# Attention inside a decoder layer: projection tiles that take every fourth token, scores and exponents in one PSUM bank, a column of ones in v

## The chip, the cores and the metric

The kernel runs on one core of a Trainium2 chip. The time is device time in microseconds (us) from the first to the last instruction and what lies around them; three runs of the kernel before took 2241.93, 2246.85 and 2247.97 us. The engines of the core are PE (TensorE, matmuls; PEld is its weight load), DVE (VectorE), ACT (ScalarE), POOL (GpSimd) and SP (SyncE, which here issues nearly all DMAs). Each runs its own instructions in order.

## The reference, cut to what matters

One decoder layer on 2048 tokens of width 1024, in float32. The change touches only the attention half of the mixer: 8 heads of 64, and for every head three branches (window, dilation) = (128,1), (512,4), (2048,16). A query at position t attends to the keys at t, t-d, t-2d, ... back to t-window.

```python
DILATED_BRANCHES = ((128, 1), (512, 4), (2048, 16))
...
def dilated_branch(q, k, v, window, dil):
...
    qs, ks, vs = to_sub(q), to_sub(k), to_sub(v)      # tokens regrouped by residue mod dil
...
    s = jnp.einsum("bnqhd,bnkhd->bnhqk", qb, kw, preferred_element_type=jnp.float32)
...
    valid = ((dist >= 0) & (dist <= L))[None] & (kpos >= 0)
    s = jnp.where(valid[None, :, None], s, -jnp.inf)
    m = jnp.max(s, axis=-1, keepdims=True)
    e = jnp.exp(s - m)
    den = jnp.sum(e, axis=-1, keepdims=True)
    p = e / den
    lse = (m + jnp.log(den))[..., 0]
    o = jnp.einsum("bnqhk,bnkhd->bnqhd", p.astype(vw.dtype), vw)
```

The three branches of a head are then combined with weights that go with their denominators. Before the attention stand an RMS norm, the projection and a gated convolution, and behind it the output projection and a SwiGLU.

## The kernel before

Every float32 operand of a matmul is split into two float16 parts, high and low, and a product is three matmuls (high by high, high by low, low by high: `mm3_steps`, L187 to L189).

The kernel has four stages in time: norm and convolution (to about 240 us of the profile), the attention (projection of the first head pair to about 306 us, then four groups g of two heads to about 845 us), the output projection, and the feed-forward, which fills the rest.

`qkv_steps(g)` projects q, k and v of the two heads of group g. It goes over the tokens in four blocks of 512 (`i`), and in each block over four tiles (`j`) of 128 consecutive tokens: 24 matmuls of 384 columns whose weights are the tile's tokens (`xh[:, k, t]`) and whose moving side are the weights of the layer. ACT copies q and k out of PSUM (L456) and the high half of v (L458), DVE makes v's low half (L459), and SP stores v to DRAM (L463, rows of 128 float16: 64 high, 64 low). After four tiles come the norms of q and k: squares on POOL (L468), a sum and a reciprocal root on DVE, two products on POOL (L473, L476), the casts to float16 on DVE (L482, L483), the low halves on POOL (L484, L485), and six DMA transposes (L195, called at L488) that put the head dimension on the partitions: `qT`, `ka` (high part of k, held twice) and `kl` (low part of k over zeros; its buffers are called kb in the profile). All have the 2048 tokens in natural order along their free dimension.

`attn_steps(g)` does the attention of the group: for each head h the branches b in the order 1, 2, 0 (dilation 4, 16, 1), in blocks u of 128 queries. A step takes either two blocks with the previous and the own block of keys (256 columns each), or four blocks with the own keys alone (128 columns each, `four`): branch 2 throughout, and the first step of branch 1. There are 152 steps, 112 of them with two blocks. A step is: score matmuls into a PSUM bank `s` (L567 with the high, L568 with the low part of k; lhsT is the queries' block, rhs a slice of the keys); on DVE the mask, the scale and the row minimum, from `s` into an SBUF tile `sm` (L572); on ACT the exponent in `sm`, with its row sum (L577); then the float16 split and the transpose of the exponents. With two blocks the split goes through `eh` (L588 on ACT, L589 on DVE) and a DMA transpose into `et` (L590, recorded at L195); with `four` PE transposes `sm` into PSUM (L583) and ACT and DVE split it from there (L584, L585). Then 12 or 24 matmuls `av` (L596) multiply by v. Slices of the keys: branch 0 contiguous; branch 1 every 4th token (`tl[:, ...:4]`, 8 bytes apart); branch 2 every 16th (`tl[:, u::16]`, 32 bytes apart). Buffers: three PSUM banks `s`, three tiles `sm`, four each of `eh` and `et`.

Order: the Tile framework derives all semaphores from the tiles and puts the instructions of each engine in an order of its own with a timeline model. `attention_pairs` feeds it the steps of group g and, between them, the projection of group g+1 (a `yield` is three matmuls; `rate` yields per step), held back by `issue_after` so that it runs at most `lag` steps ahead. In the last group the filler is the last quarter of the convolution and the first output tiles. v comes back from DRAM per head and branch in `load_v`, one DMA each, two buffers.

Of the kernel before, what the change touches and what calls it, by code (L numbers as in the profile page):

```python
# [8 lines left out]
F32 = mybir.dt.float32  # L9
# [8 lines left out]
P = 128  # L18
S = 2048
# [10 lines left out]
class Builder:  # L30
# [167 lines left out]
    def run(self):  # L198
        tc, nc, A = self.tc, self.nc, self.A
        with ExitStack() as ctx:  # L200
# [4 lines left out]
            self.d_v = [dr.tile([2, S, P], F16, name=f"d_v{g}") for g in range(4)]  # L205
# [227 lines left out]
    def qkv_steps(self, g, st):  # L433
# [12 lines left out]
        for i in range(0, NT, 4):  # L446
            f = self.at.tile([P, 4, 4, HD], F32, name="qkf", bufs=2)
            for j in range(4):
                if j % 2 == 0:
                    vs = self.at.tile([P, 2, 2, 2, HD], F16, name="vs", bufs=2)  # L450
                t = slice(j * P, (j + 1) * P)
# [3 lines left out]
                                          lambda k: wh[:, k], lambda k: wl[:, k])  # L455
                nc.scalar.activation(f[:, j].rearrange("p a b -> p (a b)"), ps[:, 0:256], AF.Copy, scale=u)  # L456
                pv = ps[:, 256:384].rearrange("p (h d) -> p h d", h=2)
                nc.scalar.activation(vs[:, j % 2, :, 0], pv, AF.Copy, scale=2.0 ** -20)  # L458
                nc.vector.scalar_tensor_tensor(vs[:, j % 2, :, 1], pv, 2.0 ** -20, vs[:, j % 2, :, 0],  # L459
                                               op0=ALU.mult, op1=ALU.subtract)  # L460
                if j % 2 == 1:
                    for h in range(2):
                        nc.sync.dma_start(dv[h, (i + j - 1) * P:(i + j + 1) * P].rearrange("(t p) c -> p t c", p=P),  # L463
                                          vs[:, :, h].rearrange("p t x d -> p t (x d)"))
            n = self.at.tile([P, 16, HD], F32, name="qkn")
            ff = f.rearrange("p a b d -> p (a b) d")
            ss = self.at.tile([P, 16], F32, name="qk_ss")
            nc.gpsimd.tensor_tensor(n, ff, ff, op=ALU.mult)  # L468
# [11 lines left out]
            for h in range(2):  # L480
                q, k = n4[:, :, h], n4[:, :, 2 + h]
                nc.vector.tensor_copy(hl[:, h, :, 0], q)  # L482
                nc.vector.tensor_copy(hl[:, 2 + h], k.unsqueeze(2).broadcast_to([P, 4, 2, HD]))  # L483
                nc.gpsimd.tensor_tensor(hl[:, h, :, 1], q, hl[:, h, :, 0], op=ALU.subtract)  # L484
                nc.gpsimd.tensor_tensor(self.klz[:, h, :, 0], k, hl[:, 2 + h, :, 0], op=ALU.subtract)  # L485
            for src, dsts in ((hl, (*qT, *ka)), (self.klz, kl)):
                for n_, dst in enumerate(dsts):
                    self.transpose(dst[:, i * P:(i + 4) * P].rearrange("p (j t) -> p j t", j=4),  # L488
                                   src[:, n_].rearrange("p j x d -> p (j x d)"))
            yield  # L490
        st.update(qT=qT, ka=ka, kl=kl)

    def attn_steps(self, g, st):
# [6 lines left out]
        def load_v(h, b):  # L500
            dv = self.d_v[g][h]
            t = V[h, b] = self.vp.tile([P, NT, P], F16, name="v", bufs=2)
# [5 lines left out]
            else:  # L508
                nc.sync.dma_start(t, dv.rearrange("(t p) c -> p t c", p=P))
        for h, b in [(h, b) for h in range(2) for b in (1, 2, 0)]:  # L510
            qT, ka, kl = (st[x][h] for x in ("qT", "ka", "kl"))
            load_v(h, b)

# [631 lines left out]
```

## Time and profile before

| what | us |
|---|---|
| three runs | 2241.93, 2246.85, 2247.97 (median 2246.85) |
| profiled execution: whole / its span | 2241.81 / 2240.0 |
| PE, DVE, ACT, POOL busy in the span | 2127.7, 1491.1, 1022.5, 670.8 |
| attention from the first score to the last av and what follows it at once (306 to 845) | 539 |
| feed-forward and what lies between | 1395 |

How to read it: the first two rows are times of whole executions, and every duration and position in this document comes from the one that was profiled. Busy shares are averages over stages with different limits, so the stage from 306 to 845 us is looked at by itself. A matmul's own duration includes its way through the pipeline; what it costs on PE is the distance from its start to the next one's.

### The profile page before, as it was taken

Reading aid. Unit: us, or ns where it says so; the run is one execution under the profiler, and the core shown is the slowest. Engines: PE = TensorE matmul, PEld = TensorE weight load, DVE = VectorE, ACT = ScalarE, POOL = GpSimd, SP = SyncE. Lnnn points to the kernel's source line nnn. Section 1 sums busy time; section 2 is a strip of 40 time slices with the busy share of each in tenths; the row PEclk is TensorE's granted clock in tenths of the full one; section 3 lists DMA queues with packets and bytes.
Section 4 is the critical chain, followed back from the end, with each engine's and each line's share of the span. In section 5 each row is a group of like instructions: output and inputs, shape, how many; then the busy total and the mean of one; then the engine's idle time right before and its main releaser. Section 6 shows DMA issues by size and latency. Waiting matters only on the chain.

```text
span 2240.0 us, 33330 instructions
## 1 busy us (share of the span) xinstructions
PE 2127.7 (95%) x11816; PEld 1067.8 (48%) x11816; DVE 1491.1 (67%) x3412; ACT 1022.5 (46%) x2390; POOL 670.8 (30%) x524
## 2 busy tenths in 40 slices
PE   4899999999899979998799999999999999999999
PEld 2344556666565644443344444444444444444444
DVE  6587557878777667785576667676767565555554
ACT  6343236666566757563343333333343343343341
POOL 0000243445434111131221122221211235555463
PEclk9999999999899989999899999999999999999999
DMA  9767356978888988869633323333223455152342
GB/s 240 160 202 254 97 123 128 184 155 161 171 159 173 233 196 245 260 198 256 170 113 104 113 82 100 107 99 104 87 93 108 164 180 179 57 192 65 115 141 94
DMA packets 569703, 339.40 MB, mean 152 GB/s; under 512 B 372928, under 2 KB 522432, under 8 KB 567104
## 3 DMA queue, kind: packets, MB, share of 16 engines
q1 hardware_dynamic: 564528, 337.20, 57.0%
q8 instruction: 92, 1.51, 0.3%
q10 hardware_dynamic: 5008, 0.08, 0.1%
q14 instruction: 75, 0.61, 0.1%
HBM read 161.04 MB, written 107.48 MB: 120 GB/s over the span
## 4 chain that ended last, share of the span: by engine, by line
PE 67%; DMA 11%; DVE 10%; ACT 4%; SPq 4%; issue 4%; POOL 0%; DVEq 0%; ACTq 0%; POOLq 0%
PE ps L949 26%; PE ps L1067 18%; PE mm L187 5%; PE mm L188 5%; PE mm L189 5%; DMA et<-eh 3%; PE s L567 3%; PE s L568 3%; SPq L195 2%; PE av L596 2%; DMA wraw<-in_w_in_dram 1%; DMA wq<-in_w_up_dram 1%; DVE vm_a L92 1%; DVE w L860 1%; DVE hl L816 1%
## 5 line engine op out<-in xcount | busy, mean ns | idle before, releaser
L949 PEld LDWEIGHTS <-w 128*128 128x128 f16 x3696 | 363.3, 98 | 469.9 <-issue 23.9
L949 PE MATMUL ps<-b,w 128*128 128x512 f16 x2112 | 467.4, 383 | 15.0 <-ACT ka L799 8.4
L1067 PE MATMUL ps<-b,w 128*128 128x512 f16 x1848 | 399.3, 380 | 0.9 <-DVE s L1085 0.8
L949 PE MATMUL ps<-hb,w 128*128 128x512 f16 x1584 | 351.4, 383 | 9.2 <-DVE s L955 8.6
L1067 PEld LDWEIGHTS <-w 128*128 128x128 f16 x1848 | 180.7, 98 | 219.4 <-issue 1.4
L577 ACT ACTIVATE sm<-sm,u 128x256 f32<-128x256 f32 (+1 forms) x384 | 173.8, 455 | 68.7 <-DVE u L572 68.2
L842 POOL TENSOR_TENSOR t<-wq 128x512 f32<-128x512 f32 (+1 forms) x46 | 59.1, 1284 | 436.1 <-issue 205.7
L955 DVE TENSOR_TENSOR s<-ps,s 128x512 f32<-128x512 f32 x220 | 150.1, 683 | 47.0 <-PE ps L949 46.5
L572 DVE CUSTOM_DVE_ANT_0 sm<-s,mask,nkap 128x256 f32<-128x256 f32 (+1 forms) x384 | 144.1, 420 | 42.9 <-PE s L568 24.7
L187 PE MATMUL mm<-wq,b 128*128 128x384 f16 x512 | 172.4, 337 | 0.0
L188 PE MATMUL mm<-wq,b 128*128 128x384 f16 x512 | 171.9, 336 | 0.0
L189 PE MATMUL mm<-wq,b 128*128 128x384 f16 x512 | 171.6, 335 | 0.0
L1074 POOL TENSOR_TENSOR x<-x,s 128x512 f32<-128x512 f32 x72 | 103.0, 1432 | 186.2 <-DVE s L1085 130.0
L1075 DVE SCALAR_TENSOR_TENSOR x<-ps,a_u,x 128x512 f32<-128x512 f32 x96 | 71.9, 749 | 112.6 <-PE ps L1067 84.1
L568 PE MATMUL s<-kb,qT 128*128 128x256 f16 (+1 forms) x384 | 131.3, 358 | 3.0 <-DMA kb<-klz 3.0
L567 PE MATMUL s<-ka,qT 128*128 128x256 f16 (+1 forms) x384 | 130.1, 355 | 3.6 <-DVE u L572 2.2
L589 DVE TENSOR_TENSOR eh<-sm,eh 128x512 f16<-128x512 f32 (+1 forms) x112 | 100.3, 898 | 40.7 <-ACT eh L588 40.0
L187 PEld LDWEIGHTS <-b 128*128 128x128 f16 x768 | 77.3, 101 | 71.7 <-ACT b L721 7.5
L188 PEld LDWEIGHTS <-b 128*128 128x128 f16 x768 | 77.3, 101 | 65.0 <-issue 6.1
L189 PEld LDWEIGHTS <-b 128*128 128x128 f16 x768 | 76.8, 100 | 65.3 <-issue 4.5
L187 PE MATMUL cvx<-b,wq 128*128 128x512 f16 (+1 forms) x200 | 76.8, 388 | 30.4 <-ACT wq L145 24.6
L859 ACT CAST w<-t 128x512 f16<-128x512 f32 x88 | 53.6, 615 | 104.7 <-PE ps L949 82.2
(298 smaller groups left out, 3705.1 us busy)
## 6 DMA issues: line engine op xcount, KB each, us to landing
d_a<-a SPq DMA_DIRECT2D x88, 256.0 KB, 2.0
d_wd<-w SPq DMA_DIRECT2D x77, 256.0 KB, 2.0
wq<-d_a SPq DMA_DIRECT2D x64, 256.0 KB, 4.3
b<-d_wd SPq DMA_DIRECT2D x14, 1024.0 KB, 5.7
wraw<-in_w_in_dram SPq DMA_DIRECT2D x24, 512.0 KB, 6.7
v<-d_v SPq DMA_DIRECT2D x24, 512.0 KB, 5.0
d_h<-hl SPq DMA_DIRECT2D x24, 512.0 KB, 4.0
wq<-in_w_gate_dram SPq DMA_DIRECT2D x22, 512.0 KB, 5.3
```

What stands on the lines that cost most here:

```text
L187: self.pe = mm(ps, lhsT=lh(k), rhs=rh(k), start=k == ks[0], stop=False)
L188: mm(ps, lhsT=lh(k), rhs=rl(k), start=False, stop=False)
L189: mm(ps, lhsT=ll(k), rhs=rh(k), start=False, stop=k == ks[-1])
L567: nc.tensor.matmul(sp[:, at[u]], lhsT=q, rhs=cols(ka, u, pv), start=True, stop=False)
L568: nc.tensor.matmul(sp[:, at[u]], lhsT=q, rhs=cols(kl, u, pv), start=False, stop=True)
L572: nc.vector.tensor_tensor_reduce(sm[:, at[u]], sp[:, at[u]], self.mask[:, P - P * has_prev(u):256], accum_out=Ub[:, u, HD + 1:HD + 2], op0 ...
L577: nc.scalar.activation(sm[:, at[u]], sm[:, at[u]], AF.Exp, scale=-1.0, bias=Ub[:, u, HD + 1:HD + 2], accum_out=Ub[:, u, HD:HD + 1])
L589: nc.vector.tensor_tensor(eh[:, w:2 * w], sm[:, 0:w], eh[:, 0:w], op=ALU.subtract)
L949: nc.tensor.matmul(ps[self.BANK[n]], lhsT=w[:, x, k], rhs=b[:, y, k], start=first and k == 0 and q == 0, stop=k == 3 and q == 2, skip_grou ...
L955: nc.vector.tensor_tensor(t, x, y, op=ALU.add)
L1067: nc.tensor.matmul(ps[self.BANK[n]], lhsT=L[n][:, x, f], rhs=B[n][:, f, y], start=first and f == 0 and q == 0, stop=f == n_f - 1 and q == ...
L1074: nc.gpsimd.tensor_tensor(o, o, s_, op=ALU.add)
```

## The change

1. **Tokens by residue.** Tile j of a block of 512 now takes the tokens j, j+4, j+8, ... (`slice(j, 4 * P, 4)`), so the tile's weights are read with a step of 4 elements. k stays in that order: in each block of 512, `ka` and `kl` hold 128 tokens of residue 0, then of residue 1, and so on. q is transposed into small tiles `qp` and put back into natural order by a DVE copy, two for each block. The slices of the keys are new (`keys`): branch 1 reads contiguous runs of 128; branch 2 reads every 4th element; branch 0 reads runs of 32, in the order of residues, and three of its blocks in each head need two matmuls for each part where there was one. Branch 0 gets a mask with its columns in the new order, and its v is loaded with the partitions in the same order, by four DMAs in place of one.
2. **Exponents in the bank.** In a step with two blocks `sm` is now `s` itself: DVE writes the masked scores back into the PSUM bank, ACT puts the exponents there, and L588 and L589 read them from there. The bank is held until L589 has ended. Steps with four blocks keep `sm` in SBUF.
3. **Ones in v.** Each half of v has 65 columns, the last 1 in the high and 0 in the low half, written once into two fixed tiles `vs`. The av matmuls have 65 columns and give the row sum too, so the exponent has no `accum_out`; rows of v in DRAM have 260 bytes in place of 256.
4. **Work moved between engines.** The squares for the norm are made on ACT straight from PSUM, 16 tiles by 4 groups, in place of POOL's 16 products; the casts of q and k to float16 go from DVE to ACT.

```diff
@@ qkv_steps
-                if j % 2 == 0:
-                    vs = self.at.tile([P, 2, 2, 2, HD], F16, name="vs", bufs=2)
-                t = slice(j * P, (j + 1) * P)
+                vs = self.vs[j // 2]
+                t = slice(j, 4 * P, 4)
...
                 nc.scalar.activation(f[:, j].rearrange("p a b -> p (a b)"), ps[:, 0:256], AF.Copy, scale=u)
+                nc.scalar.activation(n[:, 4 * j:4 * j + 4].rearrange("p a b -> p (a b)"), ps[:, 0:256], AF.Square, scale=u)
...
-            nc.gpsimd.tensor_tensor(n, ff, ff, op=ALU.mult)
...
-                nc.vector.tensor_copy(hl[:, h, :, 0], q)
-                nc.vector.tensor_copy(hl[:, 2 + h], k.unsqueeze(2).broadcast_to([P, 4, 2, HD]))
+                nc.scalar.copy(hl[:, h, :, 0], q)
+                nc.scalar.copy(hl[:, 2 + h], k.unsqueeze(2).broadcast_to([P, 4, 2, HD]))
...
-            for src, dsts in ((hl, (*qT, *ka)), (self.klz, kl)):
+            four = [self.at.tile([P, 4, P], F16, name="qp", bufs=4) for _ in range(2)]
+            for src, dsts in ((hl, (*four, *ka)), (self.klz, kl)):
...
+            for h in range(2):
+                nc.vector.tensor_copy(qT[h][:, i * P:(i + 4) * P].rearrange("p (t j) -> p t j", j=4),
+                                      four[h].rearrange("p j t -> p t j"))
@@ load_v
-            t = V[h, b] = self.vp.tile([P, NT, P], F16, name="v", bufs=2)
+            t = V[h, b] = self.vp.tile([P, NT, 2 * HD + 2], F16, name="v", bufs=2)
...
-                nc.sync.dma_start(t, dv.rearrange("(t p) c -> p t c", p=P))
+                for r in range(4):
+                    nc.sync.dma_start(t[32 * r:32 * r + 32], dv.rearrange("(n p r) c -> r p n c", n=NT, r=4)[r])
@@ attn_steps
+            def keys(tl, u, prev):
+                k = tl.rearrange("p (n j t) -> p n j t", n=4, j=4)
+                n = u // 4
+                if b == 0:
+                    m = u % 4
+                    k = k.rearrange("p n j (m t) -> p n m j t", m=4)
+                    if prev and m == 0:
+                        return [k[:, n - 1, 3], k[:, n, 0]]
+                    return [k[:, n, m - prev:m + 1]]
+                if b == 1:
+                    return [k[:, n - prev:n + 1, u % 4]]
+                return [k[:, :, u % 4, u // 4::4]]
...
-                av = self.psav.tile([P, 4, HD], F32, name="av")
+                av = self.psav.tile([P, 4, HD + 1], F32, name="av")
...
-                        pv, q = has_prev(u), cols(qT, u, 0)
-                        nc.tensor.matmul(sp[:, at[u]], lhsT=q, rhs=cols(ka, u, pv), start=True, stop=False)
-                        nc.tensor.matmul(sp[:, at[u]], lhsT=q, rhs=cols(kl, u, pv), start=False, stop=True)
-                    sm = self.ep.tile([P, 512], F32, name="sm")
+                        pv = has_prev(u)
+                        hi, lo = keys(ka, u, pv), keys(kl, u, pv)
+                        w = (at[u].stop - at[u].start) // len(hi)
+                        for x in range(len(hi)):
+                            o = sp[:, at[u].start + x * w:at[u].start + (x + 1) * w]
+                            nc.tensor.matmul(o, lhsT=query(u), rhs=hi[x], start=True, stop=False)
+                            nc.tensor.matmul(o, lhsT=query(u), rhs=lo[x], start=False, stop=True)
+                    sm = self.ep.tile([P, 512], F32, name="sm") if four else sp
...
-                        nc.scalar.activation(sm[:, at[u]], sm[:, at[u]], AF.Exp, scale=-1.0, bias=Ub[:, u, HD + 1:HD + 2],
-                                             accum_out=Ub[:, u, HD:HD + 1])
+                        nc.scalar.activation(sm[:, at[u]], sm[:, at[u]], AF.Exp, scale=-1.0, bias=Ub[:, u, HD + 1:HD + 2])
...
-                        ops = [(et[:, q * nb + x], Vb[:, kb_, o:o + HD]) for q, o in ((0, 0), (0, HD), (1, 0))
+                        ops = [(et[:, q * nb + x], Vb[:, kb_, o:o + HD + 1]) for q, o in ((0, 0), (0, HD + 1), (1, 0))
...
-                nc.scalar.copy(Ub[:, u0:u0 + 4, 0:HD], av)
+                nc.scalar.copy(Ub[:, u0:u0 + 4, 0:HD + 1], av)
@@ attention_pairs
+        for name, pattern in (("mask", [[1, P]]), ("mask4", [[1, 4], [4, 32]])):
+            mask = self.at.tile([P, 256], F32, name=name)
+            nc.gpsimd.memset(mask, 0.0)
...
+        self.vs = [self.at.tile([P, 2, 2, 2, HD + 1], F16, name=f"vs{i}") for i in range(2)]
+        for t in self.vs:
+            nc.gpsimd.memset(t[:, :, :, 0, HD:HD + 1], 1.0)
+            nc.gpsimd.memset(t[:, :, :, 1, HD:HD + 1], 0.0)
```

43 lines of the change are left out of this document (23 added, 20 removed).

## The prediction

> **What bounds the kernel now.** I read the page's busy times first, then the windows of the attention (the whole stage lies between 306 and 845 us; the change touches nothing behind it), then the chain of work in that stage, then single matmuls by shape and in the timeline. The windows' columns are the stretch, its length, busy time and count of PE, PEld, DVE, ACT and POOL, then the clock granted to PE, the share of the DMA engines and GB/s.
>
> ```profile
> PE 2127.7 (95%) x11816; PEld 1067.8 (48%) x11816; DVE 1491.1 (67%) x3412; ACT 1022.5 (46%) x2390; POOL 670.8 (30%) x524
> ```
> ```profile
> 306.00:436.00 130.00, 125.36 (x1011) 82.27 (x1010) 93.62 (x328) 78.96 (x275) 48.08 (x35) 0.96 0.76 156
> 436.00:565.00 129.00, 124.51 (x1104) 83.45 (x1103) 104.01 (x339) 84.90 (x297) 60.06 (x40) 0.96 0.85 165
> 565.00:695.00 130.00, 120.58 (x1041) 78.35 (x1040) 97.18 (x325) 79.71 (x281) 58.47 (x41) 0.91 0.84 163
> 695.00:845.00 150.00, 128.83 (x1101) 78.61 (x1099) 105.29 (x398) 94.06 (x313) 38.11 (x26) 0.92 0.94 208
> ```
> ```profile
> by line: DMA et<-eh 13.0%; PE mm L187 11.9%; PE mm L189 11.8%; PE mm L188 11.7%; PE s L567 10.5%; PE s L568 10.5%; PE av L596 7.9%; PE pt L583 3.2%; ACT sm L577 2.3%; DVE eh L589 2.0%; issue 1.9%; ACT eh L588 1.5%; DVE sm L572 1.5%; DMA r<-
> ```
> ```profile
> q1 hardware_dynamic: 258846, 93.17, 84.7%
> ```
>
> Each group takes 129 to 150 us, and PE is busy for 499 of the 539 us. It is the first bound, and the chain agrees: scores (L567, L568) hold 21% of the stage, 113 us. The second bound stands close: the DMA engines are busy for 84.7% of 539 = 456 us (last row, the queue in this window), and the wait for `et` holds 13% of the chain. DVE (400 us) and ACT (338 us) have slack.
>
> **The scores: the term that carries the sum.** In the view by shape a score of 128 columns costs more than one of 256; the timeline shows why.
>
> ```profile
> L568 PE MATMUL s<-kb,qT 128*128 128x256 f16 x216 | 68.6, 335 | 3.0 <-DMA kb<-klz 3.0
> L567 PE MATMUL s<-ka,qT 128*128 128x256 f16 x216 | 68.0, 332 | 1.4 <-DMA ka<-qkhl 1.3
> L568 PE MATMUL s<-kb,qT 128*128 128x128 f16 x168 | 63.5, 388 | 0.0
> L567 PE MATMUL s<-ka,qT 128*128 128x128 f16 x168 | 63.4, 386 | 2.2 <-DVE u L572 2.2
> ```
> ```profile
> 306.13 0.28 PE L567 MATMUL s<-ka,qT 128*128 128x128 f16 x1
> ...
> 307.05 0.34 PE L187 MATMUL mm<-wq,b 128*128 128x384 f16 x1
> ...
> 309.02 0.39 PE L567 MATMUL s<-ka,qT 128*128 128x256 f16 x1
> ...
> 309.92 0.34 PE L187 MATMUL mm<-wq,b 128*128 128x384 f16 x1
> ```
> ```profile
> 363.72 0.27 PE L567 MATMUL s<-ka,qT 128*128 128x256 f16 x1
> ...
> 364.16 0.33 PE L187 MATMUL mm<-wq,b 128*128 128x384 f16 x1
> ```
> ```profile
> 405.26 0.33 PE L189 MATMUL mm<-wq,b 128*128 128x384 f16 x1
> 405.43 0.40 PE L567 MATMUL s<-ka,qT 128*128 128x128 f16 x1
> ...
> 407.33 0.35 PE L187 MATMUL mm<-wq,b 128*128 128x384 f16 x1
> ```
>
> From start to start: branch 0 (contiguous keys) does four scores of 256 columns in 0.44 us, 0.11 each; branch 1 (8 bytes apart) four in 0.90, 0.225 each, and eight of 128 columns in 0.92, 0.115 each; branch 2 (32 bytes apart) eight of 128 in 1.90, 0.238 each. So a column costs 0.43 ns contiguous, 0.88 at 8 bytes, 1.86 at 32. The change makes branch 1 contiguous and branch 2 a walk at 8 bytes. A head has 12 blocks of 256 and 4 of 128 columns in branch 1, 16 of 128 in branch 2, two matmuls each; 8 heads:
> - branch 1: 192 x (0.225 - 0.11) = 22 us, and 64 x (0.115 - 0.055) = 4 us;
> - branch 2: 256 x (0.238 - 0.115) = 31 us.
>
> Together 57 us less on PE. Branch 0 reads runs of 64 bytes: at 1.86 ns for each separate place (branch 2's price) a run's four 16-byte pieces take 7.4 ns, its 32 columns 13.8; I take nothing, upper bound a place's price for each run, 8 x 1.86 ns x 240 matmuls = 4 us. Its split blocks are two matmuls of half the columns, also nothing.
>
> The row at 8 bytes also meets a rule that says otherwise. The Trainium skill, "Advanced Engine Details and Errata", section "SBUF Cachelines", says that lines are 16 bytes and that two hits on a line absorb the access. By it branch 1 would have run at full speed before; the trace disagrees (0.225 against 0.11). By the rule branch 2's new walk would cost 0.055 and the gain there would be 47 us, not 31.
>
> **Weight loads with a step.** The projections' 1536 loads now step by 4 elements, and branch 2's queries still step by 16.
>
> ```profile
> 405.27 0.15 PEld L567 LDWEIGHTS <-qT 128*128 128x128 f16 x1
> 363.72 0.10 PEld L568 LDWEIGHTS <-qT 128*128 128x128 f16 x1
> ```
>
> A load with the widest step takes 0.15, a contiguous one 0.10. At 405.27 the wide one lay under L189's matmul, and the next started 0.17 after it, as everywhere: a 384-column matmul hides it. Without that cover, 1536 x 0.05 = 77 us at most; I take 0. Under branch 2's new 0.115 a load of 0.15 may show: up to 256 x 0.035 = 9 us, kept for the range.
>
> **av.** 24 matmuls of 64 columns take 0.70, 29 ns each; a 65th column adds 0.43 ns x 1800 = 0.8 us.
>
> ```profile
> 407.67 0.70 PE av L596 x24
> ```
>
> **Off PE.**
>
> ```profile
> L589 DVE TENSOR_TENSOR eh<-sm,eh 128x512 f16<-128x512 f32 x104 | 95.4, 920 | 36.4 <-ACT eh L588 35.8
> L577 ACT ACTIVATION_READ_ACCUMULATOR sm<-sm,u 128x1 f32 x384 | 72.9, 190 | 0.0
> L588 ACT CAST eh<-sm 128x512 f16<-128x512 f32 x104 | 63.9, 616 | 43.3 <-DMA et<-eh 42.8
> L468 POOL TENSOR_TENSOR qkn<-qkf 128x1024 f32<-128x1024 f32 x16 | 31.2, 1948 | 51.8 <-ACT qkf L456 51.8
> L456 ACT ACTIVATE qkf<-mm,uq 128x256 f32<-128x256 f32 x64 | 29.9, 468 | 73.6 <-PE mm L189 70.2 <-POOL mask L631 3.4
> L585 DVE TENSOR_TENSOR et<-pt,et 128x512 f16<-128x512 f32 x40 | 27.4, 686 | 13.7 <-ACT et L584 13.7
> L482 DVE CAST qkhl<-qkn 128x256 f16<-128x256 f32 x32 | 23.8, 779 | 9.7 <-POOL qkn L473 9.7
> L483 DVE CAST qkhl<-qkn 128x512 f16<-128x512 f32 x32 | 18.5, 616 | 0.6 <-POOL qkn L476 0.6
> ```
>
> ACT: minus 73 (the 384 accumulator reads), plus 64 squares at L456's 0.468 = 30, plus casts 32 x 0.47 and 32 x 0.62 (L456, L588) = 35: about level. DVE: minus 42 (L482, L483), minus 104 x (0.92 - 0.69) = 24 if the split reads PSUM as fast as L585 does, plus 32 copies of q at 0.4 to 0.7 (around L483) = 13 to 22: 44 to 53 us less. POOL: minus 31. None of these is the bound; they only shorten the way from a score to its `et`. The q copy adds its 0.6 us far ahead of use, and ACT now carries casts behind which exponents queue, 0.6 us at a time. Two POOL mask selects and five memsets more before the first projection: under 2 us, beside projections.
>
> SP: load_v of branch 0 issues four DMAs for one, 8 x 3 x 0.43 = 10 us of SP's time, ahead of transposes in its queue. Rows of v grow from 256 to 260 bytes, 1.6%. The transposes, most of the DMA work, stay as they are, so 456 us of DMA work remain.
>
> ```profile
> 441.42 0.43 SPq L504 DMA_DIRECT2D v<-d_v  x1
> ```
>
> **What is late next.** If all 57 us were turned into time the stage would last 482 us and the DMA share would be 456/482 = 0.95: above the 0.94 of the busiest window. At a share of 0.90, between the stage's mean (0.85) and that window, it lasts 507 us: 32 us less. The waits that show the limit are these, behind `eh`'s four buffers and behind `et`:
>
> ```profile
> ACT eh L588 <- DMA et<-eh: 42.8, 30, 4.6
> PEld L596 <- DMA et<-eh: 27.2, 17, 7.3
> ```
>
> In the last group (0.94 already) PE's saving of 14 us can hardly show; in the other three, 43 us of PE less, DMA work of 99 to 110 us each against some 110 us of PE. I take 30 us: 2241.8 - 30 = 2212 against the profiled execution. The runs' median is 5 us above it; I add half of that: **2214**.
>
> **The bank's new hold.** The other edit that can cost: a two-block step keeps its bank until L589.
>
> ```profile
> 433.86 0.27 PE L567 MATMUL s<-ka,qT 128*128 128x256 f16 x1
> ```
> ```profile
> 440.66 2.24 DVE L589 TENSOR_TENSOR eh<-sm,eh 128x512 f16<-128x512 f32 x2
> 442.82 0.47 DVE L572 CUSTOM_DVE_ANT_0 sm<-s,mask,nkap 128x256 f32<-128x256 f32 x1
> ```
>
> Scores made at 433.86 were masked only at 442.82, when L589 had set a tile `sm` free: three `sm` already pace the mask, and scores ran up to 9 us ahead. Now the score itself waits, and behind it on PE the projections and av. A hold without queues is 0.44 + 0.9 (two L572) + 1.0 (two L577) + 0.6 + 0.7 = 3.7 us, so three banks allow a step each 1.2 us, against 539/152 = 3.5 us now. Some waits will come in bursts; they are part of what keeps the gain under 57.
>
> ```profile
> 310.54 0.48 DVE L572 CUSTOM_DVE_ANT_0 sm<-s,mask,nkap 128x256 f32<-128x256 f32 x1
> 310.66 0.51 ACT L577 ACTIVATE sm<-sm,u 128x256 f32<-128x256 f32 x1 [0.73 <-DVE u L572]
> ```
>
> Here the second block's mask ran beside the first block's exponent. The Trainium skill, "PSUM — Partial Sum Buffer", section "PSUM bank collisions raise a hardware error", wants two engines kept out of one bank at a time; no run here shows it. By it 310.66 becomes 311.0, 0.36 us more in each of 112 holds.
>
> **Rivals.** (1) *All of it shows*: transposes keep up at a share of 0.95; 2185 to 2198. For it: DVE and POOL get out of the transposes' way. Against: no window is above 0.94. Chance 0.15. (2) *The DMA side is the bound already* (PE's time goes into waits for `et`, share at 0.85 to 0.88): 456/0.87 = 524, 15 us less; 2227 to 2242. For it: 70 us of waits for `et` in the two rows above; SP's 10 us more. Chance 0.23. (3) *Slower: the ring of three banks*. If a bank is held longer than 3 x 539/152 = 10.6 us on average, the ring and not PE sets the step: at 11 us 152 x 11/3 = 557, 18 us more, 2260. For it: the step above would have held its bank 9 + 3.2 us. Against: that is a burst; a hold without queues is a third. Chance 0.11. (4) *The strides don't pay* (branch 2 bound by the load at 0.15, branch 0 at its 4 us): PE saves 44 us, and by the same share of it, 30 of 57, some 23 show: 2219, inside the forecast's own 2198 to 2228, which has 0.51.
>
> **How the numbers follow.** Range: 2190 (half of rival 1) to 2247 (all of rival 2, the near end of 3). A measurement here tells about 0.3% from no change, 6.7 us. Faster by more than that: forecast 0.51, rival 1 0.15, half of rival 2, together 0.78; same 0.12; slower 0.10.
>
> **What would show it.** Right: from start to start branch 1 at 0.11 and 0.055, branch 2 at 0.115; projections still 0.162; no accumulator reads; L589 near 690 ns; DMA share near 0.90 in the attention; more waits for `et` on PE. Wrong: waits of PE's L567 for L589 of more than 30 us in total (ring), projections above 0.17 (loads), or a stage as long as before at a share of 0.85.

## The result and the profile after

| | before | after |
|---|---|---|
| median of six runs on one chip, us | 2246.15 (2241.93 to 2247.97) | 2225.47 (2224.36 to 2226.63) |
| ratio | | 0.9911, 95% interval 0.9899 to 0.9924 |
| profiled execution: whole / its span | 2241.81 / 2240.0 | 2224.36 / 2222.6 |
| first projection matmul / first score / end of the last av, us | 240.7 / 306.1 / 835.6 | 238.9 / 287.1 / 820.0 |

The change makes the kernel 20.7 us faster. The forecast was 2214, with 2190 to 2247 as its range: the sign is right, and 11 of the 32 us of gain are missing. In the two profiled executions the difference is 17.4 us.

First the page of the changed kernel, its busy times and its main DMA queue:

```profile
PE 2081.2 (94%) x11864; PEld 1080.7 (49%) x11864; DVE 1453.5 (65%) x3380; ACT 1030.2 (46%) x2134; POOL 624.6 (28%) x515
...
q1 hardware_dynamic: 564912, 337.46, 58.3%
```

PE lost 46.5 us of busy time (2127.7 before). The span lost only 17.4, so PE's idle time in the span rose by 29.1. That is the result in one line: most of what was saved on PE came back as waiting. The next rows are windows over the attention, from the first projection to the last av: first of the kernel before, then of the kernel after (columns as in the prediction).

```profile
240.70:835.60 594.90, 559.76 (x4630) 359.86 (x4629) 427.14 (x1463) 343.55 (x1187) 229.94 (x163) 0.95 0.80 165
```
```profile
238.90:820.00 581.10, 516.58 (x4689) 373.80 (x4687) 386.55 (x1429) 352.83 (x931) 185.09 (x155) 0.95 0.86 170
```

PE's idle time is the second number minus the third: 35.1 us before, 64.5 after. DVE and POOL became lighter, and none of DVE (387 of 581 us), ACT (353) and POOL (185) is busy enough to be the new bound by itself. I count from the first projection here, and not from the first score: the framework's plan of the changed kernel puts the first score 19 us earlier, and the stretch from first score to last av, which the prediction calls the stage, would hide the gain: it is 529 us before and 533 after.

The windows of the four groups after the change:

```profile
287.00:425.00 138.00, 129.38 (x1156) 98.59 (x1155) 88.56 (x345) 88.51 (x241) 43.31 (x38) 1.00 0.78 155
425.00:555.00 130.00, 110.90 (x1063) 83.32 (x1060) 92.81 (x328) 83.24 (x222) 47.11 (x36) 0.92 0.88 168
555.00:685.00 130.00, 114.81 (x1112) 85.22 (x1110) 93.66 (x334) 88.81 (x236) 52.41 (x43) 0.96 0.93 167
685.00:830.00 145.00, 124.25 (x1127) 78.98 (x1126) 101.97 (x385) 84.00 (x210) 29.08 (x20) 0.89 0.99 214
```

PE now waits 9, 19, 15 and 21 us in them (length minus PE's busy time); before it was 5, 4, 9 and 21 in the four windows of the prediction. The waits came where PE had been full, in the first three groups. The scores in the timeline (the columns are start, duration, engine and line), at the seam between branch 1 and branch 2:

```profile
330.89 0.27 PE L597 MATMUL s<-ka,qT 128*128 128x256 f16 x1
331.00 0.27 PE L598 MATMUL s<-kb,qT 128*128 128x256 f16 x1
331.10 0.28 PE L597 MATMUL s<-ka,qT 128*128 128x128 f16 x1
...
332.06 0.34 PE L189 MATMUL mm<-wq,b 128*128 128x384 f16 x1
332.24 0.32 PE L187 MATMUL mm<-wq,b 128*128 128x384 f16 x1
332.40 0.32 PE L188 MATMUL mm<-wq,b 128*128 128x384 f16 x1
```

From start to start a 256-column score of branch 1 takes 0.11 us; the eight of branch 2 take 0.96 (331.10 to 332.06), 0.12 each; a projection takes 0.16 to 0.18, as before. Over the whole stage the medians are 0.109, 0.056, 0.120 and 0.163 us (branch 1 with 256 and 128 columns, branch 2, projections); before they were 0.229, 0.117, 0.239 and 0.163.

The groups by shape after the change (busy, mean ns, then idle time before them and what ended it):

```profile
L603 DVE CUSTOM_DVE_ANT_0 s<-s,mask,nkap 128x256 f32<-128x256 f32 x216 | 101.3, 486 | 21.0 <-PE s L598 19.7
L608 ACT ACTIVATE s<-s,u 128x256 f32<-128x256 f32 x216 | 94.7, 456 | 63.5 <-DVE u L603 46.3 <-DVE qkr_y L50 5.3 <-DVE qkr_t L48 3.1
L626 PE MATMUL av<-v,et 128*128 128x65 f16 x1800 | 80.1, 197 | 41.3 <-DMA et<-eh 25.9 <-ACT u L629 9.9 <-DMA v<-d_v 2.9
L619 DVE TENSOR_TENSOR eh<-s,eh 128x512 f16<-128x512 f32 x104 | 70.8, 686 | 39.4 <-ACT eh L618 38.8
L597 PE MATMUL s<-ka,qT 128*128 128x256 f16 x192 | 49.2, 279 | 7.5 <-DVE eh L619 6.6 <-DVE u L603 0.8
L597 PE MATMUL s<-ka,qT 128*128 128x128 f16 x216 | 46.7, 266 | 3.5 <-DVE eh L619 3.5
L603 DVE DVE_READ_ACCUMULATOR2_ANT u<- 128x1 f32 x384 | 44.4, 116 | 0.0
L496 DVE COPY qT<-qp 128x512 f16<-128x512 f16 x32 | 24.2, 759 | 37.2 <-DMA qp<-qkhl 37.2
L485 POOL TENSOR_TENSOR qkhl<-qkn,qkhl 128x256 f16<-128x256 f32 x32 | 20.9, 674 | 3.5 <-ACT qkhl L483 3.5
```

L619 is the old L589: 686 ns in place of 920. No accumulator read is left on ACT. Scores wait 10 us in all for L619 to give a bank back, and `av` waits 41 us, 26 of them for `et`. The waits in the attention:

```profile
PEld L626 <- DMA et<-eh: 34.8, 20, 5.0
PE av L626 <- DMA et<-eh: 25.9, 16, 4.5
ACT eh L618 <- DMA et<-eh: 23.2, 17, 3.7
PE s L597 <- DVE eh L619: 10.1, 11, 2.9
PE av L626 <- ACT u L629: 9.9, 8, 3.0
```

and three rows of the kernel before that the prediction does not show:

```profile
PE av L596 <- DMA et<-eh: 21.1, 13, 7.1
...
PE s L567 <- DVE u L572: 2.2, 3, 0.9
...
PE av L596 <- ACT u L599: 1.7, 4, 0.7
```

PE's 29 us of new idle time have no single owner. The wait of `av` for `et` grew by 5 us (21.1 to 25.9; on the weight loads from 27.2 to 34.8). Scores now wait 10.1 us for L619; before, they waited 2.2 for the masks. `av` waits 9.9 us for L629, the copy that empties its bank, in place of 1.7 for L599. The matmuls of L187 wait 7 us for L463 and L761, in place of 0.3. The wait of ACT's cast for a free `eh` fell, from 42.8 to 23.2, so these buffers did not become scarcer.

### The profile page after: what moved, and what is told of

Its sections match the earlier page's. It is cut to its first block, busy times and chain, and to the rows that moved or that the text cites. A ratio compares the mean times of both kernels' runs of the same rounds, so it can differ in the third digit from the quotient of the medians.

```text
span 2222.6 us, 33037 instructions
## 1 busy us (share of the span) xinstructions
PE 2081.2 (94%) x11864; PEld 1080.7 (49%) x11864; DVE 1453.5 (65%) x3380; ACT 1030.2 (46%) x2134; POOL 624.6 (28%) x515
## 4 chain that ended last, share of the span: by engine, by line
PE 54%; DVE 3%; DMA 2%; SPq 1%; ACT 1%; issue 1%; DVEq 0%; ACTq 0%
PE ps L989 32%; PE ps L1107 18%; DVE hl L856 1%; SPq L195 1%; PE mm L187 1%; PE mm L188 1%; PE mm L189 1%; DMA wq<-d_a 1%; PE ps L187 1%; PE ps L188 1%; PE ps L189 1%; DVE w L900 1%; DMA b<-b 0%; DMA wq<-in_w_up_dram 0%; DMA hb<-d_h 0%
## 5 line engine op out<-in xcount | busy, mean ns | idle before, releaser
L187 PE MATMUL mm<-wq,b 128*128 128x384 f16 x512 | 172.0, 336 | 3.7 <-DVE vs L463 3.6
L608 ACT ACTIVATE s<-s,u 128x256 f32<-128x256 f32 (+1 forms) x224 | 97.2, 451 | 67.1 <-DVE u L603 49.8
L603 DVE CUSTOM_DVE_ANT_0 s<-s,mask,nkap 128x256 f32<-128x256 f32 (+1 forms) x224 | 103.8, 481 | 24.5 <-PE s L598 20.8
L626 PE MATMUL av<-v,et 128*128 128x65 f16 x1800 | 80.1, 197 | 41.3 <-DMA et<-eh 25.9
L188 PEld LDWEIGHTS <-b 128*128 128x128 f16 x768 | 84.5, 110 | 63.9 <-issue 15.2
L187 PEld LDWEIGHTS <-b 128*128 128x128 f16 x768 | 84.4, 110 | 62.6 <-issue 5.5
L189 PEld LDWEIGHTS <-b 128*128 128x128 f16 x768 | 84.2, 110 | 57.9 <-issue 5.1
L187 PE MATMUL cvx<-b,wq 128*128 128x512 f16 (+1 forms) x200 | 76.1, 384 | 29.5 <-ACT wq L145 25.0
L597 PE MATMUL s<-ka,qT 128*128 128x128 f16 (+1 forms) x408 | 92.5, 272 | 11.0 <-DVE eh L619 10.1
L626 PEld LDWEIGHTS <-et 128*128 128x128 f16 x1800 | 73.7, 100 | 59.3 <-DMA et<-eh 34.8
L619 DVE TENSOR_TENSOR eh<-s,eh 128x512 f16<-128x512 f32 (+1 forms) x112 | 75.3, 676 | 41.3 <-ACT eh L618 40.7
```

The source lines that it names most:

```text
L187: self.pe = mm(ps, lhsT=lh(k), rhs=rh(k), start=k == ks[0], stop=False)
L188: mm(ps, lhsT=lh(k), rhs=rl(k), start=False, stop=False)
L189: mm(ps, lhsT=ll(k), rhs=rh(k), start=False, stop=k == ks[-1])
L597: nc.tensor.matmul(o, lhsT=query(u), rhs=hi[x], start=True, stop=False)
L603: nc.vector.tensor_tensor_reduce(sm[:, at[u]], sp[:, at[u]], mask[:, P - P * has_prev(u):256], accum_out=Ub[:, u, HD + 1:HD + 2], op0=ALU.add,
L608: nc.scalar.activation(sm[:, at[u]], sm[:, at[u]], AF.Exp, scale=-1.0, bias=Ub[:, u, HD + 1:HD + 2])
```

## Experiments

Question: what turns 46.5 us less on PE into 20.7? Four theories. **Ring** (theory R in the expectations): the bank held until L619 makes scores wait. **Bytes** (D): the DMA engines are full. **Queue** (S): SP issues in order, and v's loads and stores, and the heads that wait, hold up the transposes behind them. **Buffers**: four `eh` and `et` are too few. The expectations also speak of theory E, which is the whole way through `eh`, SP's queue and the transpose (Queue and Buffers together), and of theory O: PE's fixed order, with waits anywhere. The experiments ran on two other chips, each beside the kernel before on the same chip, so I compare ratios; the change itself was measured on the first chip alone. "Stage" is first projection to last av, and idle is stage minus PE busy, both from the windows of the one profiled execution of each run.

| run | median, us | ratio (95%) | stage | PE busy | idle | DMA share |
|---|---|---|---|---|---|---|
| before / after, first chip | 2246.15 / 2225.47 | 0.9911 (0.9899 to 0.9924) | 594.9 / 581.1 | 559.8 / 516.6 | 35.1 / 64.5 | 0.80 / 0.86 |
| e3 layout alone | 2227.95 | 0.9937 (0.9917 to 0.9957) | 583.1 | 511.0 | 72.1 | 0.83 |
| e4 all but the layout | 2242.80 | 1.0011 (0.9995 to 1.0027) | 599.3 | 569.3 | 30.0 | 0.80 |
| e2 no ones column | 2228.53 | 0.9941 (0.9922 to 0.9959) | 584.9 | 518.0 | 66.9 | 0.82 |
| e1 `sm` in SBUF | 2235.29 | 0.9968 (0.9954 to 0.9982) | 594.3 | 521.3 | 73.0 | 0.83 |
| e5 PE transposes in branch 1 | 2232.31 | 0.9969 (0.9957 to 0.9981) | 578.6 | 526.7 | 51.9 | 0.68 |
| e7 v once a head | 2208.63 | 0.9846 (0.9822 to 0.9870) | 561.0 | 510.4 | 50.6 | 0.77 |
| e8 the same on before | 2237.84 | 0.9992 (0.9976 to 1.0008) | 592.5 | 563.0 | 29.5 | 0.73 |
| e10 e7 with small loads | 2222.48 | 0.9914 (0.9895 to 0.9932) | 579.6 | 513.6 | 66.0 | 0.75 |
| e11 v's loads on ACT's queue | 2214.75 | 0.9880 (0.9859 to 0.9900) | 569.9 | 507.6 | 62.3 | 0.86 |
| e9 five `eh` and `et` | 2216.60 | 0.9899 (0.9879 to 0.9918) | 571.0 | 512.9 | 58.1 | 0.86 |
| e13 e9 and e11 | 2221.47 | 0.9910 (0.9891 to 0.9930) | 576.4 | 515.5 | 60.9 | 0.85 |
| e12 other lag | 2222.82 | 0.9916 (0.9899 to 0.9933) | 578.9 | 515.1 | 63.8 | 0.85 |

**Which part is the gain.** e3 is the kernel before with part 1 alone; e4 is the kernel after with part 1 undone. The core of e3, against before:

```diff
-                t = slice(j * P, (j + 1) * P)
+                t = slice(j, 4 * P, 4)
...
-            for src, dsts in ((hl, (*qT, *ka)), (self.klz, kl)):
+            for src, dsts in ((hl, (*four, *ka)), (self.klz, kl)):
...
+                return [k[:, :, u % 4, u // 4::4]]
```

> Only the first part of the change: tokens by residue, new key slices, q put back; sm in SBUF, row sum by the accumulator, squares on POOL, casts on DVE as before. PE saves the same 50 us of scores. Theory D: the gain over before is the changed kernel's own within 5 us (2220 to 2231). Theory R: with the ring gone it is faster than the changed kernel by 8 us or more (under 2218). If parts 2 to 4 carry the gain instead: over 2238.

and of e4, against after:

```diff
-                t = slice(j, 4 * P, 4)
+                t = slice(j * P, (j + 1) * P)
...
+                return [cols(tl, u, prev)]
```

> The changed kernel without its first part: tiles of consecutive tokens, keys read at 8 and 32 bytes as before; the bank kept, ones, squares and casts as changed. PE is the bound again. Theory D: within 6 us of before, 2240 to 2252, with PE busy over 2120 us. Theory R: the ring's waits now add to a full PE: 2250 to 2265. If parts 2 to 4 carry the gain: under 2232.

Windows of the stage, of e3 and of e4:

```profile
240.50:823.60 583.10, 510.99 (x4678) 369.39 (x4677) 458.02 (x1490) 341.32 (x1186) 230.43 (x166) 0.94 0.83 168
```
```profile
239.40:838.70 599.30, 569.31 (x4641) 366.20 (x4639) 364.18 (x1393) 353.92 (x930) 184.12 (x154) 0.94 0.80 165
```

Without the layout nothing is gained (1.0011); with it alone the ratio is 0.9937. What parts 2 to 4 add on the layout (0.9911) is not clear of noise, as the two intervals overlap. Laid on either base, the layout takes 49 to 53 us from PE in this stage (559.8 to 511.0, and 569.3 to 516.6) and adds 34 to 37 us of idle (35.1 to 72.1, and 30.0 to 64.5). So the idle time comes with the layout, and not with parts 2 to 4. The layout also brings work of its own, the copy of q and four loads of v for one; these two runs do not tell that from the mere fact that PE became faster. Two waits of e3 show that the new idle time need not be a wait for `et`:

```profile
PE s L597 <- DVE u L603: 18.7, 14, 3.0
PE av L627 <- DMA et<-eh: 13.9, 14, 2.6
```

`av` waits 13.9 us for `et`, less than in the kernel before (21.1), and yet PE's idle time is twice as long; scores wait 18.7 us for the masks.

e2 undoes part 3:

```diff
-                av = self.psav.tile([P, 4, HD + 1], F32, name="av")
+                av = self.psav.tile([P, 4, HD], F32, name="av")
...
+                                             accum_out=Ub[:, u, HD:HD + 1])
```

> The changed kernel without the column of ones: v rows of 256 bytes, av of 64 columns, the row sum by the exponent's accumulator again (384 accumulator reads of 0.19 us on ACT). Theory D: v's packets of 1040 and 4160 bytes took 65 and 245 ns where 1024 and 4096 took 56 and 202; with these gone the DMA work falls by some 5 us and the time moves by less than 4 us either way. Theory R: ACT's 73 us more lengthen each bank's hold by 0.2 to 0.4 us; 3 to 8 us slower than 2225.5.

```profile
241.20:826.10 584.90, 518.02 (x4689) 373.34 (x4687) 379.62 (x1425) 381.04 (x1314) 187.12 (x151) 0.94 0.82 168
```

In this window of its stage ACT is 28 us busier (381.0 against 352.8, the accumulator reads) and the DMA work falls back to 0.82 of 584.9, 480 us, in place of 500. PE's idle time stays (66.9 against 64.5): 20 us of DMA work less did not shorten the waits. The ratio, 0.9941, is 0.3% above the change's 0.9911, and the intervals overlap a little. That is some 7 us slower, the size that theory Ring had set and not theory Bytes (under 4 us), but it is hardly clear of noise.

**Ring.** e1 gives the bank back after the mask, as before the change:

```diff
-                    sm = self.ep.tile([P, 512], F32, name="sm") if four else sp
+                    sm = self.ep.tile([P, 512], F32, name="sm")
```

> The changed kernel, but masked scores and exponents of two-block steps go to an SBUF tile sm again, so a PSUM bank is free after L603 and not after L619. Theory D (the DMA engines took what PE saved): the ring of three banks costs little; the time stays within 4 us of 2225.5, DMA share in the attention stays near 0.88 to 0.99, PE's waits for L619 go (10 us) and come back as waits for et. Theory R (the ring of three banks took it): at least 8 us faster, under 2218, with PE's idle time down by as much. Either way L619's mean rises from 686 toward 900 ns, since it reads SBUF again.

It is slower than the whole change (0.9968 against 0.9911; the intervals are apart), which neither theory had expected. A row of the groups of e1, and two of its waits, show why the shorter hold doesn't pay:

```profile
L619 DVE TENSOR_TENSOR eh<-sm,eh 128x512 f16<-128x512 f32 x104 | 94.1, 908 | 42.3 <-ACT eh L618 41.8
```
```profile
ACT sm L608 <- DVE u L603: 76.3, 55, 8.1
...
PE s L597 <- DVE u L603: 23.4, 16, 6.9
```

The split takes 908 ns from SBUF and 686 from PSUM: DVE has 19 us more to do in the stage (405 against 387), and ACT waits 76 us for the masks (59 in the kernel after: 49.8 in the bank and 9.0 in SBUF). On PE, scores wait 23 us for the masks to free a bank: the bank is held for a shorter part of the step, and scores wait longer for it. So the earlier release is worth nothing by itself here. That DVE's time explains all 13 us between e1 and the change is not shown. The trace of the kernel after has the holds themselves: from a step's first score to the end of its L619, the 112 two-block steps hold their bank for 8.9 us on average (4.1 to 18.0, and 29 of them longer than 10.6). The ring is thus not the bound on average, but bursts reach it, as the 10.1 us of waiting scores show.

**Bytes or queue.** e7 loads v once for each head, 8 loads in place of 48; it leaves out the order of v's rows that branches 2 and 0 need, so its values are not the layer's. e8 is the same edit on the kernel before, where it takes out 16 loads of 24:

```diff
+            if b != 1:
+                V[h, b] = V[h, 1]
+                return
```

> The changed kernel with v loaded once for each head (branch 1's tile is used by all three branches, so the products with v of branches 2 and 0 are made with rows in another order): 40 of 48 v loads fall away, some 39 us of DMA work and 20 us of SP's issue time. Theory D (throughput of the DMA side): faster than the changed kernel by 6 us or more, ratio under 0.9885. Theory E: the transposes wait less in SP's queue, 2 to 6 us faster. Theory O: within 2 us.

> The kernel before with the same cut: v loaded once for each head, 16 of 24 loads less, some 36 us of DMA work. PE is the bound there, so all theories: within 4 us of before (ratio 0.998 to 1.002); if it gains 6 us or more, the DMA side was a bound before the change too.

Windows of the stage, of e7 and of e8:

```profile
240.70:801.70 561.00, 510.39 (x4678) 372.27 (x4677) 383.28 (x1425) 351.00 (x930) 185.48 (x154) 0.95 0.77 161
```
```profile
240.10:832.60 592.50, 563.00 (x4631) 362.64 (x4629) 426.22 (x1452) 343.73 (x1187) 233.75 (x163) 0.95 0.73 152
```

On the changed kernel the stage of the profiled execution is 20 us shorter, 14 of them idle time, and the ratio falls by 0.65%, some 15 us (0.9846 against 0.9911). By itself this would fit theory Bytes as well as Queue. On the kernel before, the smaller cut is worth nothing (0.9992), as expected where PE is the bound. The bytes and the issues of v's loads went away together, so e10 puts back 40 issues on SP, small ones, for the 40 loads of the kernel after that e7 left out:

```diff
             if b != 1:
                 V[h, b] = V[h, 1]
+                for r in range(1 if b else 4):
+                    d = self.at.tile([P, 2], F16, name="tiny", bufs=2)
+                    nc.sync.dma_start(d[0:32], dv[32 * r:32 * r + 32, 0:2])
+                    self.tiny = d
                 return
```

> The changed kernel with v loaded once for each head, as in e7_v_once (the products with v of branches 2 and 0 take rows in another order), but each of the 40 loads left out is replaced on SP's queue by a load of 32 x 4 bytes: the issues stay, the bytes and the waits for a free v buffer go. If the bytes moved are what limits the changed kernel (theory D): as e7_v_once, ratio to before 0.982 to 0.987. If SP's issue time is (theory S): back to the changed kernel's 0.990 to 0.992.

The stage of e10, its small loads (issue times in ns: least, median, most) and SP's wait for their buffers:

```profile
238.40:818.00 579.60, 513.56 (x4689) 371.75 (x4687) 390.50 (x1429) 351.27 (x930) 185.62 (x154) 0.95 0.75 155
```
```profile
L514 SPq DMA_DIRECT2D tiny<-d_v x40: 302/372/1047, 262.8 to 624.1; - x40
```
```profile
SPq L514 <- DMA tiny<-d_v: 11.1, 16, 1.5
```

The DMA work is 0.75 x 579.6 = 435 us, 65 less than in the kernel after, and yet the idle time (66.0) and the ratio (0.9914) are those of the kernel after. So fewer bytes alone do not shorten the stage. The 14 us that e7 had gained went with 40 issues, at 0.37 us each 15 us of SP, and 11.1 us in which SP waited for a small tile. This wait is a flaw of the experiment: it belongs to SP's queue too, but not to the change, so the size that e10 gives for issuing alone is an upper bound.

e11 leaves the bytes and takes the issues off SP:

```diff
-                nc.sync.dma_start(t.rearrange("p (n r) c -> p n (r c)", n=4),
+                nc.scalar.dma_start(t.rearrange("p (n r) c -> p n (r c)", n=4),
...
-                    nc.sync.dma_start(t[32 * r:32 * r + 32], dv.rearrange("(n p r) c -> r p n c", n=NT, r=4)[r])
+                    nc.scalar.dma_start(t[32 * r:32 * r + 32], dv.rearrange("(n p r) c -> r p n c", n=NT, r=4)[r])
```

> The changed kernel with its 48 v loads issued from ACT's queue: the bytes stay, some 22 us of issue time and the waits for a free v buffer leave SP's queue and come to ACT's. Theory S: faster than the changed kernel by 6 us or more, ratio under 0.9885. Theory D: ratio 0.989 to 0.993, or slower where ACT now stands still for a v buffer.

```profile
240.50:810.40 569.90, 507.60 (x4678) 369.19 (x4677) 382.55 (x1427) 351.18 (x930) 185.56 (x154) 0.96 0.86 173
```

The row is its stage. At an unchanged DMA share of 0.86 it reaches 0.9880: half of e7's extra gain without any fewer bytes, though its interval just touches that of the change. But most of its shorter stage is PE's busy time (507.6 against 516.6); idle fell by 2 us only. If the issues on SP's queue made PE wait, it is the idle time that should have fallen. Of all kernels run that keep the change's computation it has the lowest ratio: 1.2% below the kernel before.

What SP itself shows in the kernel after, in its waits and in the issues of v's loads for branch 0:

```profile
SPq L195 <- PE av L626: 46.4, 28, 4.8
...
SPq L519 <- PE pt L613: 14.2, 2, 7.4
```
```profile
L519 SPq DMA_DIRECT2D v<-d_v x32: 325/526/1717, 345.4 to 784.5; - x32
```

Twice a load of v stood at the head of SP's queue, up to 7.4 us, until PE released it, and what was queued behind it stood too. Counted from the records between 287 and 800 us, SP issued 167 plain DMAs in 112 us (before: 132 in 86) beside some 300 us of transposes; its issues, with what they wait inside, cover 416 of these 513 us (before: 387).

SP's issue time and PE's idle time do not go together, though. Over the stages, SP's issues cover 425 us before and 446 after; 394 in e7, 419 in e10, 402 in e11 and 397 in e13 (below). PE's idle time beside them is 35 and 65; 51, 66, 62 and 61. e11 and e13 took 44 and 49 us off SP, about as much as e7, and PE's idle time fell by 2 and 4 us, not by 14.

**Buffers.** e9 gives `eh` and `et` five buffers each, with two `sm` and two `qp` to make room; e13 is e9 and e11 in one:

```diff
-                    et = self.ep.tile([P, 8, P], F16, name="et", bufs=4)[:, 0:2 * nb]
+                    et = self.ep.tile([P, 8, P], F16, name="et", bufs=5)[:, 0:2 * nb]
...
-                        eh = self.ep.tile([P, 8 * P], F16, name="eh", bufs=4)[:, 0:2 * w]
+                        eh = self.ep.tile([P, 8 * P], F16, name="eh", bufs=5)[:, 0:2 * w]
```

> The changed kernel with five buffers each of eh and et in place of four (and, for room, two sm and two qp in place of three and four). A step's eh is held about 11 us from the cast to the landing of its transpose, so four allow a step each 2.8 us. Theory E with buffers as its limit: 5 us or more faster than the changed kernel, ratio under 0.989, and ACT's waits for the transposes (23 us) halve. Theories D and O, or E with SP's queue as its limit: within 3 us.

> e9_five_bufs and e11_v_on_act together: five eh and et, v loads on ACT's queue. If buffers and SP's queue both count: under 0.986 of before. If neither does: 0.988 to 0.992, as e9_five_bufs alone.

e9's 0.9899 can't be told from the change's 0.9911, and e13 (0.9910) has the gain of neither. e12 changes only how far the filler may run ahead:

```diff
-            rate, lag = (4.52, 3.49, 3.2, 2.1)[g], (12, 12, 13, 8)[g]
+            rate, lag = (4.52, 3.49, 3.2, 2.1)[g], (14, 14, 15, 10)[g]
```

> The changed kernel with the projections let two steps further ahead (lag 14, 14, 15, 10 for 12, 12, 13, 8): no work changes, only the order that the planner makes of it. Its distance from the changed kernel's 0.9911 says how much a mere change of order moves the time; I expect up to 5 us either way, 0.989 to 0.9935.

0.9916: no change. In e9 ACT's waits for a free `eh` fall to 4.6 us (23.2 with the change), and the time follows by no more than the noise. So neither buffers nor lag is shown to be a limit. Each edit also makes the framework order all engines anew; that e9 and e11 do not add up in e13 shows that differences of about 0.3% between such kernels, e11's 0.0031 among them, can't be put down to the edit's own cost.

**PE transposes for DMA transposes.** e5 takes the two-block steps of branch 1 off the DMA path:

```diff
+                pe = four or b == 1
-                    sm = self.ep.tile([P, 512], F32, name="sm") if four else sp
+                    sm = self.ep.tile([P, 512], F32, name="sm") if pe else sp
...
-                    if four:
+                    if pe:
```

> The changed kernel, but the 48 two-block steps of branch 1 go the way of the four-block steps: exponents in an SBUF sm, four transposes on PE into PSUM, split from there, no eh and no DMA transpose. 48 x 3.1 us of DMA work and 48 issues leave SP's queue; PE gets 192 transposes of 0.109 = 21 us more. Theory E (what took PE's saving is the way of the exponents through eh, SP's queue and the DMA transpose: 2.0 + 4.8 + 4.3 us a step, on PE's idle time of 64 us in the stage): faster than the changed kernel by 5 us or more, ratio to before under 0.989. Theory O (PE's order, fixed ahead, and waits anywhere): PE's 21 us show, ratio 0.996 or more.

```profile
239.60:818.20 578.60, 526.70 (x4863) 391.08 (x4862) 383.74 (x1420) 356.52 (x930) 186.04 (x153) 0.97 0.68 146
```

The window is its stage. The DMA share falls to 0.68 and idle to 51.9, while PE gets 10 us busier (526.7); the stage is 2.5 us shorter, yet the whole is slower than with the change (0.9969), as theory O had set. Of the matmuls that fill the stage, 18, some 4 us of PE, are done behind it. The rest is not explained; the stretch behind the stage takes 1399 to 1411 us, depending on the execution that was profiled, and here it took 1411. A wait removed with PE work is not a gain here.

## Why the prediction was right, and where it was off

The sign and the source of the gain were right. That 2225.47 lies in the range is in part the range's width: it reached from nearly all of the saving to none of it. Two thirds of the forecast gain came, and the step that was to say how much is the one that failed.

- **PE is the first bound, scores carry the sum: right.** e8, and e4 beside the whole change, show it from both sides. The price of the columns held: by the medians above 192 x 0.120 = 23 us, 64 x 0.061 = 4, 256 x 0.119 = 30, together 57 as forecast. In busy time the layout saved 49 to 53 us in the stage; the rest of the 57 is not accounted for.
- **Branch 2's walk at 8 bytes: 0.120 for 0.115, right.** The rule of the Trainium skill ("Advanced Engine Details and Errata", section "SBUF Cachelines") would have given 0.055 here; the trace disagrees, as it did for branch 1 before.
- **Branch 0's runs of 64 bytes and its split: nothing, right** (0.109 for 256 columns in both kernels, 0.056 for the halves).
- **Weight loads with a step stay hidden: right.** Projections have the same spacing, 0.163 us. Branch 2's step at 8 bytes lies 5 ns above the forecast, 1.3 us in all, where up to 9 were kept in the range.
- **DVE, ACT, POOL: the directions held, the sizes roughly.** In the stage DVE lost 41 us (forecast 44 to 53), POOL 45 (31 forecast; what stayed there became shorter too, L485's low half of q from 778 to 674 ns), ACT gained 9 (level). ACT's term of minus 73 us for the accumulator reads was too large: by e2 against the change they are worth 28 us of its busy time. L619 takes 686 ns, as priced from L585. Missed: the q copy takes 0.76 us, above the 0.4 to 0.7, and the accumulator read of the mask went from 82 to 116 ns.
- **"SP: 10 us", and "456 us of DMA work remain": off.** The loads of branch 0 were counted at one issue's 0.43 us; the median is 0.53 and some wait at the queue's head. The DMA work in the stage rose by 24 us (476 = 0.80 x 594.9, 500 = 0.86 x 581.1). But e10 shows that this work by itself was not what decided.
- **"What is late next": the step that failed.** It took DMA work divided by a share of 0.90 as the new length: 30 us less. From first score to the end the share came out at 0.90, as forecast (the row below, of the kernel after), but this was no confirmation. In the last group it was 0.99, and e10's stage had a share of 0.75 and nearly the same length. What grew were waits of PE on several parts of the chain from score to mask, exponent, split, transpose and `av`: 5 us more for `et`, 8 more of scores for a bank, 8 more for the copy of `av`, 7 more of L187's matmuls. Measured in place of the term of 30 us: 20.7 in the runs, 17.4 in the profiles.

```profile
287.00:830.00 543.00, 479.33 (x4449) 346.10 (x4448) 376.99 (x1390) 344.56 (x908) 171.91 (x135) 0.94 0.90 176
```

- **Rival 1 (all of it shows)**: no; two thirds to three quarters of what the layout saves on PE becomes idle time there. **Rival 2 (the DMA side)** named 2227 to 2242; 2225.47 is nearer to it than to 2214, and its sign of more waits for `et` is there, but not its cause: bytes. **Rival 3 (ring)** needed a bank held for more than 10.6 us on average, and its sign was more than 30 us of scores waiting for L619: the hold is 8.9 and the wait 10, and e1 has no gain from a shorter hold. But the prediction's own 3.7 us for a hold without queues is exceeded even by the shortest, 4.1. **Rival 4 (strides don't pay)** gave 2219, nearer than the forecast, for a reason that the medians refute.
- **The mark set for "wrong"** (scores waiting over 30 us, projections above 0.17, a stage as long as before at a share of 0.85): none was met as it stands. The third was half met: from first score to last av, as the prediction counts, the stage did stay as long (529 and 533 us), at a share of 0.90, because the first score came 19 us earlier.

Still open: why PE waits 29 us more. Bytes alone are not the reason (e10); five buffers (e9) and another lag (e12) move the time by no more than the noise. SP's queue alone is not shown to be it: e11 and e13 free SP and keep PE's idle time. Taking out loads and bytes together is worth 15 us (e7), and which of the two, or the new order of the plan, does it is not settled. A test with small loads that never wait for their buffer was not made.

## What to carry to other kernels

When the first bound gives way, do not take the share of the next resource as the new limit: list the waits of the engine that was the bound, each by what ended it. Here the largest, `av` for `et`, held 26 of 64 us and had grown by 5 of the 29. A share of busy time can land exactly where it was forecast and still not be the reason; the test is to take the work of that resource away (e10) and see whether the time moves. And a layout that makes operands contiguous is priced well by the distance from start to start of the matmuls, each layout against the other.

## What was not expected of the hardware

**The exponent now waits for both masks of its bank.** In the timeline of the kernel after:

```profile
438.75 0.48 DVE L603 CUSTOM_DVE_ANT_0 s<-s,mask,nkap 128x256 f32<-128x256 f32 x1
439.15 0.14 DVE L603 DVE_READ_ACCUMULATOR2_ANT u<- 128x1 f32 x1
439.32 0.49 DVE L603 CUSTOM_DVE_ANT_0 s<-s,mask,nkap 128x256 f32<-128x256 f32 x1
439.73 0.14 DVE L603 DVE_READ_ACCUMULATOR2_ANT u<- 128x1 f32 x1
...
439.91 0.93 ACT L608 ACTIVATE s<-s,u 128x256 f32<-128x256 f32 x2 [0.98 <-DVE u L603]
```

Both exponents start at 439.91, 0.04 us after the second mask's read has ended (439.73 + 0.14), although the first block's minimum was there at 439.29. Over the stage, in steps of two full blocks, the first exponent ran beside the second mask in 56 of 104 steps of the kernel before, in 64 of e1's 104, and in none of 104 after, where it never starts less than 0.03 us behind the second mask's read. It starts 1.17 us (median) behind its own mask's read, 0.23 before; 0.59 us of that lie between the two reads, and ACT's other work is in the rest. The Trainium skill, "PSUM — Partial Sum Buffer", section "PSUM bank collisions raise a hardware error", wants ACT and DVE kept out of one bank at a time; the trace agrees that they are kept apart, and the second mask with its read is 0.59 us of waiting, not the 0.36 worked out. Whether the chip or the framework's semaphores do it, the trace does not tell.

**Where an operand lies sets DVE's and ACT's time.** With the scores in PSUM and not in SBUF (after against e1) the split takes 686 in place of 908 ns and the exponent 456 in place of 507, while the mask's accumulator read takes 116 in place of 82.

**Stores with rows of 260 bytes land later.** The store of v in the kernel before and after (KB of one, median us from issue to landing):

```profile
d_v<-vs SPq DMA_DIRECT2D x64, 64.0 KB, 2.0
```
```profile
d_v<-vs SPq DMA_DIRECT2D x64, 65.0 KB, 4.1
```

With rows of 260 bytes the median is 3.1 us in e1, 3.3 in e4 and 3.0 in e10; with 256 bytes it is 2.0 in e2 and e3. The packets of v's loads show little of it: one of 1040 bytes takes 47 ns and one of 4160 161 in the median, against 46 and 159 for 1024 and 4096 bytes before. The means are 65 and 245 against 56 and 203, so a few packets take much longer. The Trainium skill, "DMA: Bandwidth & Descriptors", section "How a descriptor splits into AXI transactions", says that a transfer that does not start on a 256-byte boundary fetches bytes that it doesn't use; the medians of these packets do not show such a cost, and what delays the stores is open.
